# Moving one of four block subtractions from GpSimd to VectorE at the entry of a Strassen-like channel mixer

## The chip, the cores and the metric

The kernel runs on one core of one Trainium2 chip. The time is device microseconds of one execution. Before the change three runs gave 2134.68, 2135.33 and 2136.11 us, a median of 2135.33 us.

## The reference

The kernel computes a two-layer trunk over 1024 positions of width 1024. Layer 0 has a gated spatial mixer, layer 1 has chunked attention, and each layer ends with a gated channel mixer. The output is a final RMSNorm of the residual stream. The change lies in the entry of the channel mixer:

```python
def conv_ffn(h, w_in, conv_w, conv_b, w_down):
    a = h @ w_in
    C = a.shape[-1]
    a = lax.conv_general_dilated(
        a, conv_w[:, None, :].astype(a.dtype), window_strides=(1,),
        padding=[(CONV_WIDTH - 1, 0)], dimension_numbers=('NWC', 'WIO', 'NWC'),
        feature_group_count=C) + conv_b
    up, gate = jnp.split(a, 2, axis=-1)
    return (jax.nn.silu(gate) * up) @ w_down

h = h + conv_ffn(rmsnorm(h, f_norm_g[l]), f_w_in[l], f_conv_w[l], f_conv_b[l], f_w_down[l])
```

Here w_in maps the width of 1024 to 2 x 2816 channels, "up" and "gate".

## The kernel before

**Number format.** Every float32 operand of a matmul is split into a high part (rounded to the TensorE format, cast on ScalarE, L139) and a low part (the rest, a subtraction on VectorE or GpSimd, L140). A product is then three matmuls: high weight by high operand (L375), low weight by high operand (L377), high weight by low operand (L380).

**Seven products for eight.** The channel mixer computes its 2 x 2 block products in the form of Strassen and Winograd. The operand B (the normed residual) has blocks B11, B12, B21, B22: the first digit is the half of the 1024 features, the second the half of the 1024 positions. A block consists of four tiles of 128 features by 512 positions, numbered k = 0 to 3. Three products need sums of blocks: T1 = B12 - B11, T2 = B22 - T1, T3 = B22 - B12 and T4 = B21 - T2. For the weights A, with rows "up" and "gate", the sums S1 to S4 are formed per channel block j on VectorE (L390). One product is one step of twelve matmuls of 128 x 128 by 128 x 512, and seven steps make one channel block j of 128 up and 128 gate channels.

**Which step needs what.** The first channel blocks use plain block products (steps with names such as "A11", "B11"), until the sums of the operand are there. From channel block 2 on the steps are p = 1 to 7, where p = 4 uses T4, p = 5 T1, p = 6 T2 and p = 7 T3. The order is 1, 2, 6, 5, 7, 3 for block 2; then block 3's p = 1; then block 2's p = 4, which is the first step that reads T4; then block 3's 5, 6, 2, 7, 3, and so on. Results gather in PSUM in places called up and gate. Before step p = 4 of a block, ScalarE copies one half of gate to the other (L902) and VectorE adds a saved sum to it (L903); after p = 3 VectorE adds a saved sum to up (L899).

**Behind the products.** A depthwise convolution of width 3 starts on ScalarE (L831) and ends in two operations on VectorE (L833), which read PSUM; ScalarE applies silu (L838) and VectorE multiplies (L839). For each pair of channel blocks GpSimd then forms the four differences T1, T3, T2, T4 of the gated rows (L847), in this order, and SP's queue stores them (L849). The weight loads of later channel blocks (L799) are issued from the same SP queue.

**The entry.** `norm_second` (from L326) norms the second half of the positions, forms T1 and T2 in place of the residual's tiles and splits each operand. Its VectorE work stands in a block whose order is written out by hand: row by row, each row's elementwise work for k followed by the split of k - 1. Function `t2` makes, for each k, T3 (L356) and T2 (L357) on VectorE and T4 (L358) on GpSimd. The splits of T3 and T4 go on a list, `late`, from which the mixer's loop takes two at a time between its steps; the last two, those of T4 for k = 2 and 3, come behind step p = 5 of block 2. Outside the hand-ordered blocks, the order on each engine but TensorE is fixed when the kernel is built, by a planner that works from modelled times. Each engine then runs its instructions in that fixed order.

The two mixers call `norm_second` once each, so L358 runs eight times.

Of the kernel before, what the change touches and what calls it, by code (L numbers as in the profile page):

```python
# [13 lines left out]
ALU = mybir.AluOpType  # L14
# [32 lines left out]
def trunk(ctx: ExitStack, tc: tile.TileContext, x, a_win, a_wv, a_wst, a_bs, a_wout, w_kv, w_q, w_o,  # L47
          f_win, f_wdown, bias, cst, consts, fgain, out):
    nc = tc.nc
    V, S, G = nc.vector, nc.scalar, nc.gpsimd  # L50
# [15 lines left out]
    def put_off(us, fn):  # L66
        pending.append((clock[0] + us, len(pending), fn))
        pending.sort(key=lambda e: e[0])
# [64 lines left out]
    def col(c):  # L133
        return cc[:, c:c + 1]


    def split(hi, lo, src, eng=V):

        behind[S] = S.copy(hi, src)  # L139
        return eng.tensor_tensor(lo, src, f32(hi), op=ALU.subtract)  # L140
# [62 lines left out]
    def spread(r, pool, eng=None):  # L203

        bc = psS("bc")
        if eng is S:
            dg = pool.tile([P, 4, P], F32, tag="f", name="dg")
            for i in range(4):
                S.mul(dg[:, i, :], ident, r[:, i:i + 1])
            nc.tensor.matmul(bc, ones, dg.rearrange("p a b -> p (a b)"), start=True, stop=True)  # L210
            return bc

        rr = pool.tile([P, NB], F32R, tag="st", name="rr")
        split(rr[:, 0:4], rr[:, 4:8], r[:, 0:4])
        for n in range(2):
            dg = pool.tile([P, 4, P], F32R, tag="f", name="dg")
            V.tensor_tensor(dg, ident.unsqueeze(1).broadcast_to([P, 4, P]),
                            f32(rr[:, 4 * n:4 * n + 4]).unsqueeze(2).broadcast_to([P, 4, P]), op=ALU.mult)
            nc.tensor.matmul(bc, ones_r, dg.rearrange("p a b -> p (a b)"), start=n == 0, stop=n == 1)
            tick()  # L220
        return bc
# [20 lines left out]
    def rstd_rows(acc, pool, then, cs=slice(0, H)):  # L242

        pt = psS("pm")
        sums = [acc[0][:, cs], *([acc[1][:, cs]] if len(acc) > 2 and cs.start else []), *acc[2:]]
        n = (cs.stop - cs.start) // P
        for k, a in enumerate(sums):
            for i in range(n):
                nc.tensor.matmul(pt[:, i:i + 1], a[:, i * P:(i + 1) * P], ones[:, 0:1], start=k == i == 0,
                                 stop=k == len(sums) - 1, skip_group_check=True)  # L250
                tick(0)
        then(rstd_of(pt[:, :n], n, pool))
# [73 lines left out]
    def norm_second(h, acc, gain, X, wait=3.6):  # L326

        def scale(r):
            bc = spread(r, npl, S)

            def ys_of(k):
                return [[h[i][:, hs] for hs in halves] for i in (k, k + 4)]

            def part(n, k, new, y, eng=V):
                X[n][k] = b = new()
                split(*b, y, eng)

            def row(work, parts):

                for k, fn in enumerate(work):  # L340
                    fn(k)
                    if k:
                        parts(k - 1)
                parts(len(work) - 1)

            def scaled(k):
                y = h[k][:, halves[1]]
                V.scalar_tensor_tensor(y, y, col(gain + k), bc, op0=ALU.mult, op1=ALU.mult)

            def t1(k):  # L350
                (y11, y12), _ = ys_of(k)
                V.tensor_tensor(y11, y12, y11, op=ALU.subtract)

            def t2(k):
                (y11, y12), (y21, y22) = ys_of(k)
                V.tensor_tensor(y12, y22, y12, op=ALU.subtract)  # L356
                V.tensor_tensor(y22, y22, y11, op=ALU.subtract)  # L357
                G.tensor_tensor(y21, y21, y22, op=ALU.subtract)  # L358

            with tc.manual_schedule(engines={mybir.EngineType.DVE}):  # L360
                row([scaled] * KD, lambda k: part("B22" if k >= 4 else "B12", k % 4, new_y if k >= 4 else new_t,
                                                  h[k][:, halves[1]], G if k % 2 else V))
                row([t1] * 4, lambda k: part("T1", k, new_y, ys_of(k)[0][0]))
                row([t2] * 4, lambda k: part("T2", k, new_t, ys_of(k)[1][1]))
            late.extend(lambda k=k: part("T3", k, new_t, ys_of(k)[0][1]) for k in range(4))
            late.extend(lambda k=k: part("T4", k, new_t, ys_of(k)[1][0]) for k in range(4))
        put_off(wait, lambda: rstd_rows(acc, npl, lambda r: put_off(3.2, lambda: scale(r))))
# [1264 lines left out]
```

## Time and profile before

| what | value |
| --- | --- |
| median of three runs | 2135.33 us |
| span of the profiled execution, first to last instruction | 2131.1 us |
| TensorE busy | 2116.7 us, 99% |
| VectorE busy | 1545.7 us, 73% |
| ScalarE busy | 1065.4 us, 50% |
| GpSimd busy | 752.9 us, 35% |
| mean granted TensorE clock | 0.998 |
| L358 on GpSimd | 8 operations, 27.0 us |

The profile is of one execution. Its engines are PE (TensorE matmuls), PEld (weight loads of TensorE), DVE (VectorE), ACT (ScalarE), POOL (GpSimd) and SP (the queue of transfers). Times in a timeline are microseconds from the start of the span. An entry "[2.72 <-DVE gate L903]" means that the engine stood idle 2.72 us and that VectorE's operation of line 903 ended this. The first channel mixer's entry lies near 300 to 370 us, the second's near 1485 to 1560 us. Spans on GpSimd are rough; they include time in which an operation has started and does not get on.

### The profile page before, as it was taken

To read this page: it belongs to the slowest core of one execution; us is meant where nothing else is said; L and a number is where in the kernel's file an instruction comes from. 1 tells how busy PE (TensorE), PEld (TensorE's weight loads), DVE (VectorE), ACT (ScalarE), POOL (GpSimd) and SP (SyncE) were. 2 spreads that over 40 slices of the span, in tenths; PEclk is the share of its full clock that TensorE was granted. 3 is DMA by queue.
4 is the path that set the end of the run, shared out by engine and by line. 5 is a ranking of instruction groups with operands and counts; after the bars stand their busy time and mean duration, and the time that the engine had idled before them with its cause. 6 is when DMAs were issued, how large, how long until landed. Compare 5 with 4: busy or idle time off the path is not lost.

```text
span 2131.1 us, 28842 instructions
## 1 busy us (share of the span) xinstructions
PE 2116.7 (99%) x9944; PEld 1773.0 (83%) x9944; DVE 1545.7 (73%) x2311; ACT 1065.4 (50%) x1878; POOL 752.9 (35%) x530
## 2 busy tenths in 40 slices
PE   9999999999999999999999999999999999999998
PEld 8888877888888888888888888888888888888887
DVE  4188789888888856675665655665988888885576
ACT  6333555545455544555555555643545544454443
POOL 1075745242333412054545444421322323341020
PEclk9999999999999999999999999999999999999999
DMA  7257722354445976735554555663243545478653
GB/s 253 79 203 256 243 99 99 130 193 138 163 165 194 296 269 215 239 105 139 139 127 129 129 130 133 178 218 114 73 154 134 186 137 175 164 278 300 213 190 126
DMA packets 181450, 367.86 MB, mean 173 GB/s; under 512 B 42908, under 2 KB 43292, under 8 KB 181304
## 3 DMA queue, kind: packets, MB, share of 16 engines
q1 hardware_dynamic: 177128, 358.47, 51.8%
q10 hardware_dynamic: 4176, 7.55, 1.0%
q8 instruction: 78, 1.28, 0.3%
q14 instruction: 68, 0.56, 0.1%
HBM read 233.12 MB, written 103.40 MB: 158 GB/s over the span
## 4 chain that ended last, share of the span: by engine, by line
PE 93%; DVE 4%; POOL 1%; ACT 1%; issue 1%; DMA 0%; DVEq 0%; SPq 0%; POOLq 0%; ACTq 0%
PE up L995 10%; PE gate L995 10%; PE up L375 7%; PE up L377 7%; PE up L380 7%; PE gate L375 5%; PE gate L377 5%; PE gate L380 5%; PE vps L510 4%; PE qkv L184 4%; PE qkv L181 4%; PE qkv L188 4%; PE ups L181 1%; PE po L1290 1%; PE st L1256 1%; PE ups L184 1%
## 5 line engine op out<-in xcount | busy, mean ns | idle before, releaser
L140 DVE TENSOR_TENSOR wlo<-raw,whi 128x512 fp32r<-128x512 f32 (+1 forms) x395 | 343.7, 876 | 179.8 <-ACT whi L139 179.6
L139 ACT CAST whi<-raw 128x512 fp32r<-128x512 f32 (+1 forms) x395 | 245.0, 623 | 282.7 <-PE gate L995 198.5
L375 PE MATMUL up<-yh,whi 128*128 128x512 f32 x688 | 267.8, 389 | 0.0
L377 PE MATMUL up<-yh,wlo 128*128 128x512 f32 x688 | 267.8, 389 | 0.0
L1270 POOL TENSOR_TENSOR pl<-p,ph 128x640 fp32r<-128x640 f32 (+4 forms) x128 | 161.1, 1261 | 180.1 <-ACT ph L1269 134.4
L847 POOL TENSOR_TENSOR h<-a 128x512 f32<-128x512 f32 x44 | 80.6, 1832 | 398.7 <-DVE a L839 387.3
L375 PE MATMUL gate<-th,whi 128*128 128x512 f32 x496 | 193.9, 391 | 2.7 <-DVE gate L903 2.7
L377 PE MATMUL gate<-th,wlo 128*128 128x512 f32 x496 | 193.9, 391 | 0.0
L380 PE MATMUL up<-yl,whi 128*128 128x512 f32 x688 | 184.2, 389 | 0.0
L380 PEld LDWEIGHTS up<-yl,whi 128*128 128x128 f32 x688 | 129.2, 188 | 27.2 <-POOL yl L140 0.5
L375 PEld LDWEIGHTS up<-yh,whi 128*128 128x128 f32 x688 | 129.2, 188 | 27.1 <-ACT gate L886 0.3
L377 PEld LDWEIGHTS up<-yh,wlo 128*128 128x128 f32 x688 | 129.2, 188 | 26.8
L140 DVE TENSOR_TENSOR yl<-raw,yh 128x512 fp32r<-128x512 f32 x172 | 143.1, 834 | 8.4 <-ACT yh L139 8.2
L184 PE MATMUL qkv<-yh,wlo 128*128 128x512 f32 x336 | 134.3, 400 | 0.0
L380 PE MATMUL gate<-tl,whi 128*128 128x512 f32 x496 | 132.7, 389 | 0.0
L181 PE MATMUL qkv<-yh,whi 128*128 128x512 f32 x336 | 132.5, 394 | 0.0
L139 ACT CAST whi<-S 128x512 fp32r<-128x512 f32 x160 | 99.0, 619 | 65.0 <-PE up L380 59.0
L140 DVE TENSOR_TENSOR wlo<-S,whi 128x512 fp32r<-128x512 f32 x160 | 130.2, 814 | 0.0
L995 PE MATMUL up<-yl,whi 128*128 128x512 f32 (+1 forms) x312 | 120.6, 387 | 0.0
L995 PE MATMUL up<-yh,whi 128*128 128x512 f32 (+1 forms) x312 | 120.4, 386 | 0.0
L995 PE MATMUL gate<-yh,wlo 128*128 128x512 f32 (+1 forms) x312 | 120.4, 386 | 0.0
L995 PE MATMUL up<-yh,wlo 128*128 128x512 f32 (+1 forms) x312 | 120.3, 386 | 0.0
(306 smaller groups left out, 5274.6 us busy)
## 6 DMA issues: line engine op xcount, KB each, us to landing
raw<-in_f_win SPq DMA_DIRECT2D x88, 512.0 KB
gT<-h SPq DMA_DIRECT2D x88, 256.0 KB
h<-in_f_wdown SPq DMA_DIRECT2D x44, 512.0 KB
dS<-h SPq DMA_DIRECT2D x88, 256.0 KB
raw<-dS SPq DMA_DIRECT2D x40, 512.0 KB
raw<-gT SPq DMA_DIRECT2D x40, 512.0 KB
gB<-a SPq DMA_DIRECT2D x66, 256.0 KB
raw<-in_f_wdown SPq DMA_DIRECT2D x30, 512.0 KB
```

Of the source, the lines that this page charges most:

```text
L139: behind[S] = S.copy(hi, src)
L140: return eng.tensor_tensor(lo, src, f32(hi), op=ALU.subtract)
L181: nc.tensor.matmul(ps, wh[:, k, :], xs[k][0], start=k == 0, stop=False)
L184: nc.tensor.matmul(ps, wl[:, k, :], xs[k][0], start=False, stop=False)
L188: nc.tensor.matmul(ps, wh[:, k, :], xs[k][1], start=False, stop=k == last)
L375: nc.tensor.matmul(ps, wh[:, k, :], xs[k][0], start=first and k == 0, stop=False, skip_group_check=True)
L377: nc.tensor.matmul(ps, wl[:, k, :], xs[k][0], start=False, stop=False, skip_group_check=True)
L380: nc.tensor.matmul(ps, wh[:, k, :], xs[k][1], start=False, stop=k == 3, skip_group_check=True)
L510: nc.tensor.matmul(ps, a, b, start=k == i == 0, stop=k == KD - 1 and i == 2)
L847: G.tensor_tensor(B[n], x, B.get(y) if isinstance(y, str) else y, op=ALU.subtract)
L995: nc.tensor.matmul(ps[:, cs], w[:, ms], x[:, cs], start=q == i == 0 and p in (1, 6, 5, 4), stop=q == NP - 1 and i == 2, skip_group_check=True)
L1270: marks[2] = G.tensor_tensor(pl[:, :n], pf[:, :n], f32(ph[:, :n]), op=ALU.subtract)
```

## The change

T4 of the last tile, k = 3, is subtracted on VectorE. Those of k = 0, 1 and 2 stay on GpSimd. Since `t2` is called inside the hand-ordered block, the new VectorE operation stands directly behind T2's of k = 3 (L357) and ahead of the splits of T2 for k = 2 and k = 3. Nothing else is edited.

```diff
                 V.tensor_tensor(y12, y22, y12, op=ALU.subtract)
                 V.tensor_tensor(y22, y22, y11, op=ALU.subtract)
-                G.tensor_tensor(y21, y21, y22, op=ALU.subtract)
+                (V if k == 3 else G).tensor_tensor(y21, y21, y22, op=ALU.subtract)
```

## Prediction, made before the changed kernel was run

> **What bounds the kernel now.** I read the page's busy shares first, then the waits of TensorE (PE) over the whole run (engine, line, what it waited for; total, times, longest).
>
> ```profile
> span 2131.1 us, 28842 instructions
> PE 2116.7 (99%) x9944; PEld 1773.0 (83%) x9944; DVE 1545.7 (73%) x2311; ACT 1065.4 (50%) x1878; POOL 752.9 (35%) x530
> ...
> PE gate L375 <- DVE gate L903: 2.7, 1, 2.7
> PE gate L249 <- DVE acc L238: 1.0, 1, 1.0
> ```
>
> TensorE is busy nearly all the time, so a change can only win what TensorE waits, plus what its clock loses over a wait. One wait stands out, and it is in the stage that this change edits: it lies in the first channel mixer, before VectorE's L903. The chain of waits around it (start, length, what) leads back to the changed line, L358:
>
> ```profile
> 342.76 8.32 POOL h L358
> ...
> 355.25 0.62 PE gate L375
> ```
>
> The timeline of each engine (start, length, engine, line, operation; in brackets the idle time before it and who ended it) gives the way from the one to the other.
>
> ```profile
> 333.37 5.76 POOL L358 TENSOR_TENSOR h<-h,h 128x512 f32<-128x512 f32 x1 [1.39 <-DVE h L357]
> 342.71 8.36 POOL L358 TENSOR_TENSOR h<-h,h 128x512 f32<-128x512 f32 x1
> ...
> 345.15 0.62 ACT L139 CAST th<-h 128x512 fp32r<-128x512 f32 x1
> 351.10 0.62 ACT L139 CAST th<-h 128x512 fp32r<-128x512 f32 x1 [5.33 <-POOL h L358]
> 352.15 0.58 ACT L902 COPY gate<-gate 128x512 f32<-128x512 f32 x1
> ...
> 349.24 0.69 DVE L390 TENSOR_TENSOR S<-raw,S 128x512 f32<-128x512 f32 x1
> 351.75 1.14 DVE L140 TENSOR_TENSOR tl<-h,th 128x512 fp32r<-128x512 f32 x1 [1.83 <-ACT th L139]
> 352.82 1.77 DVE L140 TENSOR_TENSOR wlo<-raw,whi 128x512 fp32r<-128x512 f32 x1
> 354.51 0.69 DVE L903 TENSOR_TENSOR gate<-gate,h 128x512 f32<-128x512 f32 x1
> 355.11 1.18 DVE L140 TENSOR_TENSOR wlo<-S,whi 128x512 fp32r<-128x512 f32 x1
> 356.21 0.69 DVE L899 TENSOR_TENSOR up<-up,h 128x512 f32<-128x512 f32 x1
> ```
>
> The subtraction of k = 3, the one that moves, sits 8.36 us on GpSimd (POOL). ScalarE stands 5.33 us in front of the cast of its result, and behind that cast in ScalarE's queue stand a weight cast and L902, the turn of the gate's sums. VectorE stands 1.83 us, then does the low part, a weight's low part and L903, and only then may TensorE take the product of T4. TensorE's own rows, and windows with its busy time, granted clock, DMA share and GB/s in the last columns:
>
> ```profile
> 349.65 0.39 PE L375 MATMUL up<-yh,whi 128*128 128x512 f32 x1
> 355.25 0.62 PE L375 MATMUL gate<-th,whi 128*128 128x512 f32 x1 [2.72 <-DVE gate L903]
> 359.69 0.40 PE L375 MATMUL up<-yh,whi 128*128 128x512 f32 x1
> 367.86 0.39 PE L375 MATMUL gate<-th,whi 128*128 128x512 f32 x1
> ...
> 293.00:296.40 3.40, 2.58 (x15) 2.32 (x16) 2.00 (x4) 0.36 (x2) 1.02 (x1) 1.00 0.12 25
> 355.25:359.00 3.75, 3.75 (x10) 2.93 (x10) 2.93 (x5) 1.20 (x1) 0.48 (x1) 0.54 0.81 247
> ```
>
> From 359.69 to 367.86 lie three products, 2.72 us each. The product of T4 should therefore start at 349.65 + 2.72 = 352.37 and the next at 355.09. It starts at 355.25 and the next at 359.69. **The stall costs 359.69 - 355.09 = 4.60 us**: 2.88 us of waiting and 1.72 us because the product behind it runs at a granted clock of 0.54. The wait of 1.0 us at L249 cost no clock: its window shows 1.00.
>
> **Why GpSimd takes 8.36 us.** The same kind of operation, beside other work of VectorE:
>
> ```profile
> L358 POOL TENSOR_TENSOR h<-h,h x8: 1633/2277/8361, 325.0 to 1522.5; 128x512 f32<-128x512 f32 x8
> ...
> 340.00:350.00 10.00, 10.00 (x46) 8.26 (x45) 9.93 (x15) 5.16 (x10) 10.00 (x2) 1.00 0.12 45
> ...
> 336.09 0.69 DVE L357 TENSOR_TENSOR h<-h,h 128x512 f32<-128x512 f32 x1
> 337.89 1.28 DVE L833 SCALAR_TENSOR_TENSOR a<-gate,cc,a 128x1023 f32<-128x1023 f32 x1
> 340.29 1.29 DVE L140 TENSOR_TENSOR tl<-h,th 128x512 fp32r<-128x512 f32 x2
> 347.50 1.22 DVE L839 TENSOR_TENSOR a<-a 128x1024 f32<-128x1024 f32 x1
> ...
> 351.04 1.31 POOL L847 TENSOR_TENSOR h<-a 128x512 f32<-128x512 f32 x1
> 352.31 3.42 POOL L847 TENSOR_TENSOR h<-a,h 128x512 f32<-128x512 f32 x2
> ```
>
> VectorE is busy 9.93 of 10 us there. The subtraction of k = 2 (333.37) ends at 339.13, together with L833 (337.89 to 339.17), whose source lies in PSUM; the one of k = 3 ends 1.1 us after VectorE fell idle at 349.93. So GpSimd gets through while VectorE does not read two SBUF operands, and needs 1.1 to 1.2 us of such time. The reverse shows too: the weight's low part at 352.82 takes 1.77 us in place of 0.69 while L847 runs.
>
> **The change, part by part.** *Removed*: GpSimd's operation of k = 3, twice in the run (once per mixer). No DMA hangs on it. ScalarE's cast at 351.10 can then follow the one at 345.15, at 345.7, and L902 waits only for TensorE's product of T3, which ends two products ahead of the natural start of T4's: 352.37 - 2 x 2.72 = 346.93.
>
> *Added*: one subtraction on VectorE behind L357 of k = 3. The same kind, L357, takes 0.69 us and the next instruction follows 0.60 later; I take 0.60. VectorE's stream from there to 349.93 has no gap, so everything behind it moves by 0.60. Two things feel it.
>
> First, the low part of T2's k = 3 (first of the two at 340.29) ends at 341.58 in place of 340.98. TensorE wants it for the last of these four matmuls, at 340.56 + 3 x 0.23 = 341.25:
>
> ```profile
> 340.56 1.08 PE L380 MATMUL gate<-tl,whi 128*128 128x512 f32 x4
> ```
>
> With 0.04 us from a VectorE end to a matmul (355.20 to 355.25) that is a **new wait of 0.37 us**; the bounds are 0 (the stream recovers) and 0.60 (no slack at all). It is too short for the clock, by the 1.0 us row.
>
> Second, L903. VectorE reaches 349.84 (349.24 + 0.60), does the sum S, the low part of T4's k = 3, a weight's low part, and starts L903 at 349.84 + 3 x 0.60 = 351.64, ending 352.33. TensorE, 0.37 later than its rhythm, wants it at 352.74: no wait, with 0.4 us to spare. The bounds are a wait of 0 and of 0.8 (two more instructions of 0.60 in front).
>
> *What is late next*: GpSimd's three differences of L847 (T3, T2, T4 of the gated rows) now meet the full VectorE. T3 needs L839, which ends at 349.3. It comes through during L903 (source in PSUM), 351.7 to 352.8, T2 during L899, which follows L903 by one weight's low part (the rows at 355.11 and 356.21), about 353.4 to 354.5, T4 when VectorE next runs dry, by 356.9. SP's queue issues T3's store and, behind it, a weight load:
>
> ```profile
> 352.37 0.32 SPq L849 DMA_DIRECT2D gT<-h  x1
> 354.61 0.33 SPq L799 DMA_DIRECT2D raw<-in_f_win  x1
> ...
> 358.90 0.69 DVE L390 TENSOR_TENSOR S<-raw 128x512 f32<-128x512 f32 x1 [0.82 <-DMA raw<-in_f_win]
> 363.69 0.68 DVE L140 TENSOR_TENSOR wlo<-S,whi 128x512 fp32r<-128x512 f32 x1
> ```
>
> The load is issued at about 353.2, 1.4 earlier, and S starts at 357.5; the weight at 363.69 follows 4.79 later and ends at 363.0. TensorE wants it at 367.86 - 4.23 + 0.23 = 363.9. It holds, with 0.9 us; bounds 0 and 0.5 of wait.
>
> *The second mixer* has the operation too:
>
> ```profile
> 1522.47 2.28 POOL L358 TENSOR_TENSOR h<-h,h 128x512 f32<-128x512 f32 x1 [1.32 <-DVE h L357]
> ...
> 1523.65 2.18 DVE L839 TENSOR_TENSOR a<-a 128x1024 f32<-128x1024 f32 x1
> 1540.63 0.69 DVE L903 TENSOR_TENSOR gate<-gate,h 128x512 f32<-128x512 f32 x1
> ...
> 1542.31 0.39 PE L375 MATMUL gate<-th,whi 128*128 128x512 f32 x1
> ```
>
> There TensorE never waits: L903 ends at 1541.32, 0.99 us ahead of need. VectorE gains 0.96 (L839 takes 2.18 beside GpSimd, 1.22 alone) and pays 0.60. Its cover is those 0.99 us, so the term is 0, with bounds 0 and 0.6.
>
> **Sum**: -4.60 + 0.37 = **-4.23 us**. The span goes from 2131.1 to 2126.9. The runs' median lies 4.2 above the span, and I carry that over: 2135.33 - 4.23 = 2131.1. A change of 0.2% (4.27 us) is about what a measurement of this kernel can tell from none, and the forecast lies on that line.
>
> **Rivals.**
>
> *The clock did not drop in the timed runs.* The 1.72 us come from one execution. Only one wait in the middle of the run lost clock, so how often a gap of 2.88 us does so isn't shown; the runs' spread of 1.4 us has about this size. Then the gain is 2.88 - 0.37 = 2.5: 2132.8. The Trainium skill, "TensorE: Matmul & The Clock Gate", section "What's actually happening", gives a free-running window of about 3.4 us and half rate after an idle one; by it a gap of 2.88 us would drop the clock only in some positions, which speaks for this rival, while the row here shows that it did drop.
>
> *GpSimd takes the port in between.* If T3, ready at 349.3, gets in at the next instruction boundary and T2 behind it, each holds VectorE for 1.14 us (1.77 - 0.69 shows 1.08). L903 ends at 354.6 in place of 352.33, TensorE waits 1.9: 2133.0, or 2134.7 with a clock loss. For it: the stretched rows at 351.75 and 352.82. Against: the whole 7.2 us up to 349.93, in which GpSimd waited at every boundary. The Trainium skill, "SBUF — State Buffer", section "Who interferes with whom", has whoever issues first hold the pair for a whole instruction; it names no right of VectorE to keep it over a run of instructions, as the trace shows.
>
> *The stall moves ten us on.* If T3 gets nothing during L903 and L899, it waits until VectorE runs dry at about 354.7 and ends at 355.9; the load behind it in SP's queue is issued at 356.0 and lands at 360.2, the weight is ready at 365.6 in place of 363.0, and TensorE waits 365.6 - 363.9 = 1.7: 2132.8. Against: L903 reads PSUM as L833 does.
>
> *Slower.* The order outside the hand-ordered blocks is laid by a planner from modelled times, and the edit changes these. If it puts L903 behind the two weights' low parts that now follow it, GpSimd's three differences hold VectorE there: 351.64 + 2 x 0.60 + 3 x 1.14 = 356.3, against 354.51 now, 1.8 us worse than before; in the second mixer, laid by the same planner, 4.6 - 0.99 = 3.6 us of new wait and 1.7 of clock. Together 7.1: 2142.4. It decides from the point where L903 of the first mixer starts after 354.51. For it: VectorE has no slack here. Against: L903 hangs on an event of TensorE that is not moved.
>
> *It does nothing.* If another wait stands right behind the one removed (L902 or the load of a weight), the time stays within 1 us of 2135.3. Against: no row shows one.
>
> **How the numbers follow.** Forecast 0.55, clock 0.12, port 0.09, moved stall 0.08, nothing 0.06, slower 0.10. The forecast's own gain, from its bounds, is 3.2 to 4.8. The line of 4.27 us lies inside it: 0.40 of its 0.55 I put beyond it, since the new wait of 0.37 has a bound at 0 and VectorE's other terms err to both sides. So faster 0.40, slower 0.10, and within 0.2% the remaining 0.15 of the forecast and the four cases of less gain, 0.50. The range of 8 in 10 leaves out the slower case and a little of the last one, and reaches 1.1 us below the forecast for the bounds and the runs' spread: 2130.0 to 2135.4.
>
> **What would show it.** Right: no operation of L358 on GpSimd from 340 on; ScalarE's casts of T4 without the 5.33 us; L903 of the first mixer ending near 352.3; no TensorE wait over 1 us there and a granted clock of 1.00 through 350 to 360; a wait of some 0.4 us at L380 near 341. Wrong: L903 after 353, a TensorE wait near 364, L847 starting long before L903 and VectorE rows of 1.7 us around it, or a wait in the second mixer near 1542.

## The result, and the profile after

The changed kernel takes **2131.62 us**, the median of 11 runs (2130.22 to 2133.61). Eleven runs of the kernel before, taken with them, have a median of 2135.33 us. The ratio is 0.9979, with a 95% interval of 0.9971 to 0.9988, which is 2.6 to 6.2 us less. The two medians differ by 3.71 us. The forecast was 2131.1, the range 2130.0 to 2135.4.

The page's first lines, and the waits of TensorE over the whole run after the change (engine, line, what it waited for; total, times, longest):

```profile
span 2129.5 us, 28843 instructions
PE 2116.1 (99%) x9944; PEld 1771.8 (83%) x9944; DVE 1546.9 (73%) x2313; ACT 1066.3 (50%) x1878; POOL 744.6 (35%) x528
...
PE gate L249 <- DVE acc L238: 1.0, 1, 1.0
...
PE up L375 <- ACT gate L886: 0.6, 1, 0.6
...
PE gate L380 <- DVE tl L140: 0.2, 1, 0.2
```

The wait of 2.7 us before L903 is gone. One at L380 is new, and it is the only one left between 320 and 420 us. The rest of the difference lies outside the changed stage; the largest new row there, 0.6 us at L886, is taken up below.

To measure the stage itself, take the first matmul of block 2's p = 1 (330.58 before) and the first of block 3's p = 5 (359.69 before). Between them lie nine products, and 9 x 2.72 = 24.48 us is their length without a wait. TensorE's timeline, first before, then after the change (start, length, engine, line, operation; in brackets the idle time ahead of it and what ended it):

```profile
330.58 0.39 PE L375 MATMUL up<-yh,whi 128*128 128x512 f32 x1
```

```profile
331.71 0.39 PE L375 MATMUL up<-yh,whi 128*128 128x512 f32 x1
...
342.78 0.50 PE L380 MATMUL gate<-tl,whi 128*128 128x512 f32 x1 [0.25 <-DVE tl L140]
...
354.02 0.39 PE L375 MATMUL gate<-th,whi 128*128 128x512 f32 x1
...
356.74 0.39 PE L375 MATMUL up<-yh,whi 128*128 128x512 f32 x1
```

The stage took 359.69 - 330.58 = 29.11 us before and takes 356.74 - 331.71 = 25.03 us after, **4.08 us less**. What is left above 24.48 is 0.55 us, nearly all of it at L380. (The stage starts 1.13 us later in this execution; a second execution of the kernel before starts it at 333.06, later still, so the start differs from execution to execution. Places in the stage are compared from its start.)

VectorE's, ScalarE's, GpSimd's and SP's timelines around the place where the stall was:

```profile
349.26 1.21 DVE L839 TENSOR_TENSOR a<-a 128x1024 f32<-128x1024 f32 x1
350.40 0.67 DVE L390 TENSOR_TENSOR S<-raw,S 128x512 f32<-128x512 f32 x1
351.00 1.28 DVE L140 TENSOR_TENSOR tl<-h,th 128x512 fp32r<-128x512 f32 x2
352.20 0.67 DVE L140 TENSOR_TENSOR wlo<-raw,whi 128x512 fp32r<-128x512 f32 x1
352.80 0.68 DVE L903 TENSOR_TENSOR gate<-gate,h 128x512 f32<-128x512 f32 x1
353.40 1.19 DVE L140 TENSOR_TENSOR wlo<-S,whi 128x512 fp32r<-128x512 f32 x1
354.52 0.68 DVE L899 TENSOR_TENSOR up<-up,h 128x512 f32<-128x512 f32 x1
355.12 1.19 DVE L140 TENSOR_TENSOR wlo<-S,whi 128x512 fp32r<-128x512 f32 x1
356.24 1.79 DVE L140 TENSOR_TENSOR wlo<-raw,whi 128x512 fp32r<-128x512 f32 x1
358.58 0.69 DVE L390 TENSOR_TENSOR S<-raw 128x512 f32<-128x512 f32 x1 [0.55 <-DMA raw<-in_f_win]
...
347.25 1.15 ACT L139 CAST th<-h 128x512 fp32r<-128x512 f32 x2
...
348.81 0.59 ACT L902 COPY gate<-gate 128x512 f32<-128x512 f32 x1
...
350.61 3.44 POOL L847 TENSOR_TENSOR h<-a 128x512 f32<-128x512 f32 x1 [4.90 <-DVE a L839]
354.01 3.47 POOL L847 TENSOR_TENSOR h<-a,h 128x512 f32<-128x512 f32 x2
...
354.08 0.32 SPq L849 DMA_DIRECT2D gT<-h  x1
354.49 0.38 SPq L799 DMA_DIRECT2D raw<-in_f_win  x1
```

ScalarE's two casts of T4 stand together at 347.25 with no idle time, and L902 comes at 348.81 in place of 352.15. VectorE runs on without a gap. L903 ends at 353.48, 0.54 us ahead of the product at 354.02. GpSimd's L847 stands from 350.61 and gets on only with L903; the stretched rows of VectorE (1.19, 1.19, 1.79) all lie behind L903. The window from 351.00 to 354.50, in which the stall would have come, has TensorE busy 3.50 of 3.50 us at a granted clock of 1.00.

**Where the rest is.** The stage wins 4.08 us, but the spans of the two profiled executions differ by 1.6 only. Outside the stage, waits of half a microsecond come and go. The largest such step after the change, on TensorE:

```profile
1753.25 0.50 PE L375 MATMUL up<-yh,whi 128*128 128x512 f32 x1 [0.56 <-ACT gate L886]
```

VectorE had waited 3.65 us for a weight's transfer just ahead of it. This lies nearly 200 us behind the second mixer's entry. The second executions below speak against the edit as its cause: the kernel before has a wait of 0.42 us at this row's place in its second one (1758.74), and the changed kernel has none in its second. Outside the stage (span less stage) the two executions of the kernel before take 2102.0 and 2106.2 us, the two of the changed kernel 2104.5 and 2104.8. So two spans can't judge a change of 4 us. One small cost is the edit's: the stretch of the second mixer from block 2's p = 1 to the T4 product's low parts behind it. Its first matmul starts at 1490.63 before and 1488.09 after, the last row of low parts at 1563.18 before and 1560.82 after. That is 72.55 us before and 72.73 after, 0.18 longer, with no wait on any matmul's row.

### The profile page after: what moved, and what is told of

It is laid out like the page before. It is cut to its first block, busy times and chain, and to the rows that moved or that the text cites. A ratio compares the mean times of both kernels' runs of the same rounds, so it can differ in the third digit from the quotient of the medians.

```text
span 2129.5 us, 28843 instructions
## 1 busy us (share of the span) xinstructions
PE 2116.1 (99%) x9944; PEld 1771.8 (83%) x9944; DVE 1546.9 (73%) x2313; ACT 1066.3 (50%) x1878; POOL 744.6 (35%) x528
## 4 chain that ended last, share of the span: by engine, by line
PE 93%; DVE 4%; ACT 1%; issue 1%; DMA 0%; POOL 0%; SPq 0%; DVEq 0%; POOLq 0%; ACTq 0%
PE up L995 10%; PE gate L995 10%; PE up L375 7%; PE up L377 7%; PE up L380 7%; PE gate L375 5%; PE gate L380 5%; PE gate L377 5%; PE vps L510 4%; PE qkv L184 4%; PE qkv L181 4%; PE qkv L188 4%; PE ups L181 1%; PE po L1290 1%; PE st L1256 1%; PE po L1288 1%
## 5 line engine op out<-in xcount | busy, mean ns | idle before, releaser
L847 POOL TENSOR_TENSOR h<-a 128x512 f32<-128x512 f32 x44 | 82.0, 1864 | 403.3 <-DVE a L839 390.7
L380 PE MATMUL up<-yl,whi 128*128 128x512 f32 x688 | 184.2, 389 | 0.0
L380 PEld LDWEIGHTS up<-yl,whi 128*128 128x128 f32 x688 | 129.1, 188 | 27.3 <-POOL yl L140 0.5
L380 PE MATMUL gate<-tl,whi 128*128 128x512 f32 x496 | 132.8, 389 | 0.2 <-DVE tl L140 0.2
```

Of the source, the lines that this page charges most:

```text
L380: nc.tensor.matmul(ps, wh[:, k, :], xs[k][1], start=False, stop=k == 3, skip_group_check=True)
L847: G.tensor_tensor(B[n], x, B.get(y) if isinstance(y, str) else y, op=ALU.subtract)
```

## The experiments

Each comparison below is with runs of the kernel before on the same chip. "Stage" is the length defined above: 29.11 us before, 25.03 after. "Second stretch" is that of the second mixer: 72.55 and 72.73.

**One mixer at a time.** L358 runs in both mixers; these two kernels make the edit in one of them only.

```diff
-                (V if k == 3 else G).tensor_tensor(y21, y21, y22, op=ALU.subtract)
+                (V if k == 3 and gain == C_FG else G).tensor_tensor(y21, y21, y22, op=ALU.subtract)
```

> T4 of k = 3 goes to VectorE in the first mixer only. If the gain comes from the stall before L903 in the first mixer (my theory), the whole gain is here: 3.7 to 4.1 us below the kernel before, a wait of about 0.4 us at L380 near 342 us, no wait before L903. If the changed order in the second mixer brings part of it (rival), the gain is smaller by over 1 us.

```diff
-                (V if k == 3 else G).tensor_tensor(y21, y21, y22, op=ALU.subtract)
+                (V if k == 3 and gain != C_FG else G).tensor_tensor(y21, y21, y22, op=ALU.subtract)
```

> T4 of k = 3 goes to VectorE in the second mixer only; the first mixer is as before. My theory: no gain, within 0.7 us of the kernel before, and the stall of 2.7 us with its half-rate clock is still there in the first mixer. Rival (the second mixer shares in the gain, or pays part of it back): 1 us or more to either side, with a TensorE wait that appears or disappears after 1490 us.

The first mixer alone: 2131.07 us against 2135.78, ratio 0.9977 [0.9968, 0.9986]; stage 25.03, second stretch 72.56. The second alone: 2135.58 against 2135.78, ratio 0.9995 [0.9986, 1.0004]; stage 29.12, second stretch 72.72, and TensorE waits 2.7 us for L903 as of old.

The whole gain is in the first mixer. The second mixer's half of the edit is worth nothing; the traces show it 0.16 to 0.20 us slower in all three executions that have it, and the times can't tell that from zero.

**Is it the engine or the order?** The theory says that GpSimd's last T4 was not slow in itself, but held off by VectorE for as long as no instruction let it through. Then GpSimd can keep the operation if it only comes ahead of L847's T1, so that it meets L833, which reads PSUM. Every other engine's order is that of before.

```diff
-                G.tensor_tensor(y21, y21, y22, op=ALU.subtract)
+                behind["t4"] = G.tensor_tensor(y21, y21, y22, op=ALU.subtract)
...
-                G.tensor_tensor(B[n], x, B.get(y) if isinstance(y, str) else y, op=ALU.subtract)
+                with tc.issue_after(behind["t4"].ins) if j == 1 and n == "T1" else ExitStack(): G.tensor_tensor(B[n], ...)
```

> All four T4 stay on GpSimd. Only two GpSimd instructions change places: T4 of k = 3 in front of T1 of the gated rows (L847). Every other engine keeps its order. Port theory: T4 then starts at about 339.1 and ends with the convolution step of VectorE at 342.7, ScalarE's wait of 5.3 us is gone and so is the stall of 4.6 us; T1 is held off in its place until L903, SP's store of T1 delays the weight load behind it, and TensorE waits 0.8 us (0 to 1.5) one weight later, near 363: a gain of 3.8 us (3.1 to 4.6). Rival (the gain needs VectorE's new order, or the operation itself is slow on GpSimd): the stall stays, a gain under 1 us.

2133.14 us against 2135.78, ratio 0.9985 [0.9976, 0.9995]. TensorE's, GpSimd's and VectorE's rows:

```profile
332.49 0.39 PE L375 MATMUL up<-yh,whi 128*128 128x512 f32 x1
...
356.99 0.39 PE L375 MATMUL up<-yh,whi 128*128 128x512 f32 x1
...
366.10 0.50 PE L377 MATMUL gate<-th,wlo 128*128 128x512 f32 x1 [0.56 <-DVE wlo L140]
...
368.77 0.39 PE L375 MATMUL up<-yh,whi 128*128 128x512 f32 x1
...
335.33 9.36 POOL L358 TENSOR_TENSOR h<-h,h 128x512 f32<-128x512 f32 x2 [1.38 <-DVE h L357]
344.66 9.60 POOL L847 TENSOR_TENSOR h<-a 128x512 f32<-128x512 f32 x1
...
343.46 1.27 DVE L833 SCALAR_TENSOR_TENSOR a<-gate,cc,a 128x1022 f32<-128x1022 f32 x1
```

The stage is 356.99 - 332.49 = 24.50 us: the stall is gone without moving anything to VectorE. T4 of k = 3 ends at 344.69, with L833 (343.46 to 344.73), and now T1 of L847, the same kind of operation, is held for 9.60 us in its place. Nothing on TensorE waits for T1, but SP's queue does: the weight load behind T1's store comes late, and the product with the wait at 366.10 takes 3.62 us (365.15 to 368.77) in place of 2.72, 0.90 more, about as expected. Another 0.96 us at 396.75 was not expected; the second execution of the changed kernel loses 0.50 at the same matmul, so its cause stays open. The stage wins 29.11 - 24.50 = 4.61, and 2.75 is left of that, as the medians say (2.64); the gain expected was 3.1 to 4.6. The cause of the stall is settled all the same: the held operation, not GpSimd's own work, and it matters only which operation is the one that is held.

**Behind the splits.** The forecast's new wait at L380 comes from the low part of T2 that the added subtraction pushes back. Here the subtraction stands behind T2's splits and ahead of T4's.

```diff
-                (V if k == 3 else G).tensor_tensor(y21, y21, y22, op=ALU.subtract)
+                k < 3 and G.tensor_tensor(y21, y21, y22, op=ALU.subtract)
...
-                row([t2] * 4, lambda k: part("T2", k, new_t, ys_of(k)[1][1]))
+                row([t2] * 4, lambda k: part("T2", k, new_t, ys_of(k)[1][1])); V.tensor_tensor(ys_of(3)[1][0], *ys_of(3)[1], op=ALU.subtract)
```

> T4 of k = 3 on VectorE as in the changed kernel, but behind the low part of T2's k = 3 in place of ahead of it. If the 0.4 us wait at L380 is the price of the 0.6 us put in front of that low part, the wait is gone and the gain is 4.6 us, 0.4 to 0.5 more than the changed kernel's, L903 still in time. If the wait has another cause, it stays at 0.4 us.

2130.92 us against 2135.78, ratio 0.9974 [0.9964, 0.9984]. TensorE and VectorE:

```profile
332.90 0.39 PE L375 MATMUL up<-yh,whi 128*128 128x512 f32 x1
342.88 1.08 PE L380 MATMUL gate<-tl,whi 128*128 128x512 f32 x4
...
357.61 0.39 PE L375 MATMUL up<-yh,whi 128*128 128x512 f32 x1
...
342.66 0.68 DVE L140 TENSOR_TENSOR tl<-h,th 128x512 fp32r<-128x512 f32 x1
343.27 0.68 DVE L364 TENSOR_TENSOR h<-h,h 128x512 f32<-128x512 f32 x1
```

The four matmuls of L380 run without a gap, and the stage is 24.71 us, 0.32 less than in the changed kernel, where 0.4 to 0.5 was expected; the second stretch is 72.54. What is left above 24.48 lies at the product of T4: L903 ends at 354.70, and the product starts at 354.76, 0.1 late. So VectorE's spare time ahead of L903 is used up. The two stretches together are 0.5 us shorter than in the changed kernel. That is below what the times can tell; the kernel is clearly faster than the kernel before.

**More blocks.** If VectorE's stream has room, more of T4 could move: k = 2 and 3, or all four.

```diff
-                (V if k == 3 else G).tensor_tensor(y21, y21, y22, op=ALU.subtract)
+                (V if k >= 2 else G).tensor_tensor(y21, y21, y22, op=ALU.subtract)
```

> T4 of k = 2 and k = 3 on VectorE, both ahead of the low part of T2's k = 3. Theory: two times 0.60 us in front of that low part, a wait of 0.9 to 1.0 us at L380 near 342 in place of 0.37, no stall before L903: 3.5 us faster than the kernel before, 0.6 slower than the changed one. Rival (GpSimd relieved further is a gain in itself): faster than the changed kernel.

2133.53 us against 2136.70, ratio 0.9988 [0.9978, 0.9997]. TensorE's waits from 320 to 420, VectorE's and GpSimd's rows, and a window with its granted clock (0.62) ahead of the last two columns:

```profile
PE gate L380 <- DVE tl L140: 1.9, 2, 1.2
...
336.74 1.80 DVE L140 TENSOR_TENSOR tl<-h,th 128x512 fp32r<-128x512 f32 x1
...
336.37 1.63 POOL L847 TENSOR_TENSOR h<-a 128x512 f32<-128x512 f32 x1 [3.87 <-DVE a L839]
...
344.60:348.30 3.70, 3.69 (x10) 2.88 (x11) 3.70 (x6) 3.10 (x5) 0.00 (x0) 0.62 0.03 7
```

The waits at L380 are 1.9 us, about twice what I had expected. GpSimd, relieved of k = 2, is free when L839 ends, gets the port, and stretches a low part from 0.68 to 1.80. In this execution one of the waits also cost a piece of half clock, and the stage is 29.09, no shorter than before. The median is 3.2 us lower all the same, near the 3.5 that was expected, but this trace doesn't show where: the profiled execution took 2133.06 us because it was quick outside the stage (2102.0 us, like the first one of the kernel before). If both kernels spend alike outside, most timed runs had a shorter stage than this one; how often the clock drops there isn't shown. The agreement with the 3.5 is of the number, not of the mechanism.

```diff
-                (V if k == 3 else G).tensor_tensor(y21, y21, y22, op=ALU.subtract)
+                V.tensor_tensor(y21, y21, y22, op=ALU.subtract)
```

> All four T4 on VectorE. Theory: four times 0.60 us in front of the low part, 2.4 - 0.23 = a wait of about 2.2 us at or before L380 near 342, with a half-rate clock behind it if the gap is seen: 0.7 to 2.4 us faster than the kernel before. Rival (the port relieved for good): as fast as the changed kernel or faster.

2139.77 us against 2136.70, ratio 1.0013 [1.0004, 1.0023]: 3.1 us **slower** where 0.7 to 2.4 faster was expected, a miss. TensorE's waits from 320 to 420, and a window:

```profile
PE gate L380 <- DVE tl L140: 2.2, 2, 1.7
PE gate L375 <- ACT th L139: 2.0, 1, 2.0
...
350.00:354.00 4.00, 4.00 (x10) 3.10 (x10) 4.00 (x7) 2.14 (x4) 1.23 (x1) 0.50 0.13 47
```

Three waits for T2's parts, 4.2 us together, come in place of the one at L903, the clock is halved for 6.83 us from 347.26 on, and the stage is 32.09. The second mixer waits 1.3 us at L380 as well. I had counted 0.60 us for each further operation. But the last T2 (L357 of k = 3) comes 4.80 us later in the stage than in the kernel before (343.67 - 333.36 against 336.09 - 330.58), and three further operations are only 1.8 of these. The rest is other VectorE work that now stands ahead of it, in an order that the planner chose. VectorE runs without a gap here, so the stage can take little more than one operation of 0.60 us.

**A gap in the port.** The sharpest test of the port: leave T4 on GpSimd, and put one more VectorE operation that reads PSUM into VectorE's stream while T4 is held. It should let T4 through there.

```diff
-            late.extend(lambda k=k: part("T4", k, new_t, ys_of(k)[1][0]) for k in range(4))
+            late.extend(lambda k=k: (part("T4", k, new_t, ys_of(k)[1][0]), k == 0 and gain == C_FG and V.tensor_tensor(psum["gate"][1][:, 0:H], psum["gate"][1][:, 0:H], ys_of(0)[1][0], op=ALU.add)) for k in range(4))
```

> All four T4 stay on GpSimd and GpSimd's order stays. VectorE gets one more instruction in the first mixer, of no use: like L903 it reads one operand from PSUM and one from SBUF, on a PSUM place that is overwritten before it is read again, behind the low part of T4's k = 0. Port theory: GpSimd's T4 of k = 3, held off since 342.7, gets through beside it, ends at about 347.5 in place of 351.0, VectorE pays 0.60 for the instruction and up to 0.55 for the one behind it, L903 ends at 352.9 against a need at 352.4: a wait of about 0.5 us in place of 2.9, and 4.0 us faster than the kernel before, by work added. Rival (GpSimd is slow for another reason): T4 still ends at 351 or later, L903 is no earlier, and the kernel is 0 to 0.6 us slower.

2137.37 us against 2135.74, ratio 1.0008 [0.9999, 1.0016]. GpSimd, VectorE (L366 is the added operation), ScalarE, TensorE, and the window behind the wait:

```profile
345.44 4.81 POOL L358 TENSOR_TENSOR h<-h,h 128x512 f32<-128x512 f32 x1
352.68 1.63 POOL L847 TENSOR_TENSOR h<-a 128x512 f32<-128x512 f32 x1 [2.43 <-DVE a L839]
...
349.02 0.69 DVE L366 TENSOR_TENSOR gate<-gate,h 128x512 f32<-128x512 f32 x1
349.62 1.18 DVE L140 TENSOR_TENSOR tl<-h,th 128x512 fp32r<-128x512 f32 x1
...
353.07 1.80 DVE L390 TENSOR_TENSOR S<-raw,S 128x512 f32<-128x512 f32 x1
354.79 1.77 DVE L140 TENSOR_TENSOR tl<-h,th 128x512 fp32r<-128x512 f32 x1
356.48 1.75 DVE L140 TENSOR_TENSOR wlo<-raw,whi 128x512 fp32r<-128x512 f32 x1
358.15 0.69 DVE L903 TENSOR_TENSOR gate<-gate,h 128x512 f32<-128x512 f32 x1
...
350.28 0.62 ACT L139 CAST th<-h 128x512 fp32r<-128x512 f32 x1 [1.78 <-POOL h L358]
...
358.89 0.80 PE L375 MATMUL gate<-th,whi 128*128 128x512 f32 x1 [3.64 <-DVE gate L903]
...
358.89:362.50 3.61, 3.61 (x10) 2.90 (x11) 2.33 (x4) 1.21 (x1) 0.00 (x0) 0.60 0.76 226
```

The first half is as expected. T4 comes through beside L366, in 4.81 us in place of 8.36, the row behind L366 is stretched to 1.18, and ScalarE waits 1.78 in place of 5.33. The second half is not (4.0 us faster was expected, and the interval includes no change at all): T3, T2 and T4 of L847 then get the port one after the other between VectorE's instructions, each of the three rows ahead of L903 takes 1.75 to 1.80 us, and TensorE waits 3.64 for L903. That is the rival "GpSimd takes the port in between" of the prediction, real in this kernel though not in the changed one.

**Second executions**, to see what repeats: the kernel before, the gap, and the changed kernel.

> The kernel before, unchanged, for a second trace. If the half-rate clock follows from the 2.9 us gap every time, the stall costs 4.6 us again with one half-rate stretch. If it depends on where the gap falls, it costs between 2.9 and 4.6 us. Steps of up to 0.7 us elsewhere against the first trace are differences from execution to execution, and show what of the small steps between the traces of before and after is not due to the change.

> The kernel of e8 once more, for a second trace. In e8 GpSimd's three differences (L847) got the port between VectorE's instructions from 353 on and stretched three of them by 1.1 us each; in the changed kernel they waited for L903. If this belongs to the order of the instructions, the same three rows are 1.75 us or longer again and TensorE waits 3.4 to 3.8 us before L903; if it is chance in the arbitration, other rows are stretched, or none, and the wait is 0.3 to 2.5 us.

> The changed kernel once more, for a second trace. If the order decides who gets the port, VectorE's rows between the second L839 and L903 of the first mixer last 0.67 us each again, and the wait at L380 near 342 is 0.25 us of record (0.47 us of delay), with no wait before L903. If it is chance, L903 can be late by 1.1 us or a multiple, and the changed kernel has executions with a stall.

The kernel before: 2137.46 us, stage 29.15, second stretch 72.56, a wait of 2.8 us at L903 with a granted clock of 0.54 behind it. It also has waits elsewhere that its first profile lacks (0.31 us near 219, 0.79 near 1567, 0.42 near 1759). The wait of 1.0 us at L249, which cost no clock in the first profile, does here. Its window:

```profile
296.00:299.80 3.80, 3.80 (x11) 2.97 (x10) 0.28 (x2) 1.89 (x5) 1.02 (x1) 0.55 0.47 138
```

The gap again: 2134.52 us, with the same three stretched rows (1.79, 1.78, 1.75) and the same wait of 3.64. Both executions of this order agree, and so do all three of the changed kernel's order in the first mixer, so it is the order of the instructions that decides who gets the port here, and hardly chance. The clock did **not** drop this time, and the stage is 28.46 in place of 29.78. TensorE's row and the window behind it:

```profile
357.58 0.50 PE L375 MATMUL gate<-th,whi 128*128 128x512 f32 x1 [3.64 <-DVE gate L903]
...
357.58:361.00 3.42, 3.42 (x15) 2.84 (x16) 2.34 (x4) 1.51 (x2) 0.00 (x0) 1.00 0.79 241
```

The changed kernel: 2131.90 us, stage 25.03, second stretch 72.75, the wait of 0.2 at L380, no stretched row ahead of L903. It repeats to 0.02 us.

## Why the prediction was right, point by point

**The stall and its cause: right.** It was put at 4.60 us. The stage was 29.11 - 24.48 = 4.63 us over its length without a wait, and all of this but the new wait at L380 is gone. The cause, GpSimd's operation held off by VectorE's stream, is shown by two experiments that leave the operation on GpSimd: earlier in GpSimd's order it is not held past L833, and with a PSUM-reading operation put beside it, it comes through there. The chain from it through ScalarE's cast and L902 to L903 holds as well: in the gap kernel, ScalarE's wait shrank with it (5.33 to 1.78).

**The new wait at L380: right in kind, sized too small.** Forecast 0.37 us, bounds 0 and 0.60. The three matmuls ahead of it start at 341.69 and follow each other at 0.23, so the last was due at 341.69 + 3 x 0.23 = 342.38; it starts at 342.78, 0.40 late. But the next matmul then follows 0.34 later (343.12) in place of 0.23: TensorE takes another 0.11 to get going again, which the forecast left out. Together some 0.5 us.

**"Too short for the clock, by the 1.0 us row": the number held, the reason didn't.** The clock stayed at 1.00 behind this wait. But the 1.0 us row at L249 is no proof: the same wait halved the clock in 4 of the 12 profiled executions. I read a rule from one execution; what decides is worked out in the last section.

**L903 in time: right.** Forecast: its end 21.75 us from the stage's start (352.33 - 330.58), no wait. Measured: 353.48 - 331.71 = 21.77, with 0.54 to spare.

**What is late next: right.** T3 of L847 came with L903, T2 with L899. T4 came 0.5 us earlier than "when VectorE runs dry", stretching the low part at 356.24 to 1.79. The load was to be issued 22.6 us from the stage's start and S to start at 26.9; measured 22.8 and 26.9. The weight behind it caused no wait.

**The second mixer: 0 forecast, 0.18 measured**, inside its bounds of 0 and 0.6. No matmul's row shows a wait; two products take 2.77 and 2.85 us in place of 2.72. Why isn't settled. L839 takes 1.23 us, as forecast, but VectorE now waits 0.66 us ahead of it for ScalarE's silu (L838), a wait that the forecast left out. L903 ends 0.80 us ahead of need (1539.03 for 1539.83) in place of 0.99, and still causes no wait.

**The sum.** -4.60 + 0.37 = -4.23 forecast; in the traces -4.08 in the stage and +0.18 in the second mixer, -3.90; the medians differ by 3.71, the ratio says 4.5 with an interval of 2.6 to 6.2.

**Span and median.** The prediction carried over that the median lay 4.2 us above the profiled span. In every later run, of any of these kernels, the execution's own time is 1.8 to 2.6 us above its span, 2.1 in the middle. So the other 2.1 of the 4.2 meant that the profiled execution of before was itself a quick one, at about 2133.2. The predicted span of 2126.9 was therefore too low (2129.5), while the predicted median came out right because the shift was applied to the median.

**The rivals.** *The clock did not drop in the timed runs*: three profiled executions with a gap of 2.7 to 2.9 us all dropped, so 2.9 us alone isn't what was won; but a 3.64 us gap did and did not, so the 1.72 us are a likelihood, not a constant. By the limit worked out in the last section, 2.08 of the 2.88 us would have to lie in one piece of 3.41 us. If every position is equally likely, that is so about six times in ten (an estimate), so the rival was likelier than its 0.12. *GpSimd takes the port in between*: not here, but in the gap kernel. *The stall moves on*: not here; in the kernel with GpSimd's order changed it does, at 0.90 us. *Slower by the planner*: it did lay VectorE's instructions otherwise ahead of L903 (four low parts stand together at 342.05, and the last two of T4 at 351.00), but L903 kept its place. *Nothing*: the experiment with the first mixer alone rules it out.

**Open.** T3 of L847 starts 0.14 us behind L839's end in both kernels, yet in the changed kernel it loses every boundary up to L903, and in the gap kernel it wins the second. The orders of VectorE behind L839 are S, low, low, weight, L903 in the one and low, S, low, weight, L903 in the other. In the kernel with two blocks moved, T1 wins the first boundary behind its start too. Why the order decides was not settled.

## What to carry to other kernels

When an operation on GpSimd takes several times its usual length, ask first what VectorE was doing beside it: reordering GpSimd's own queue, so that the operation meets a VectorE instruction that reads PSUM, removed the same stall as moving the work did. Moving one operation of 0.60 us onto an engine that runs without a gap pays if it ends a wait of several us, and the next three of the same kind made the kernel slower: count the slack of what stands behind the new place, operation by operation. Put the moved operation behind what is needed first, and judge the edit by the length of its own stage, since half-microsecond waits elsewhere hid more than 2 us of 4 in the span.

## What the runs showed of the hardware that was not expected

**The clock.** In the middle of a run, a halved stretch lasted 3.41 us wherever it came, or twice that (6.83, in the kernel with four blocks moved). Whether a gap brings one is not set by its length alone: 2.7 to 2.9 us dropped 3 of 3 times, 3.64 us 1 of 2, and the wait of 1.0 us 4 of 12. The clock records of the twelve traces, read together, show what does. Counted from the clock's first rise, 3.9 to 10.2 us into the span, every drop starts at a whole multiple of 3.413 us. So the run is cut into pieces of this length, and they fall on the program differently in each execution. Count 0.227 us of work from the start of a matmul of 512 columns (the distance of two of them), and less for fewer columns in proportion. Then work fills 4% to 38.8% of the ten pieces just ahead of a drop, and 39.0% or more of each of some 7400 other pieces at full clock (the ends of a run aside: in a first piece, 29% brought no drop). The 3.64 us gap dropped the clock when 3.13 us of it lay in one piece, and not when 1.92 and 1.72 lay in two. Behind the wait of 1.0 us stand eight matmuls of one column (L249, 0.9 us); the clock dropped in just the four executions in which the wait and these matmuls lay in one piece. The limit was found in these traces and has been tried on no others.

The Trainium skill, "TensorE: Matmul & The Clock Gate", section "What's actually happening", has a free-running window of 3413 ns, and the traces agree with that length; its condition of a whole idle window they don't bear out, since 1.0 us of waiting was enough four times. Nor can a gap of 2.88 us fill a window of that length, so the prediction's "only in some positions" doesn't follow from that condition; it follows from the pieces above. Halved stretches, which cost 1.6 us behind L249 and 1.7 behind L903, probably make much of the spread of the runs. Of 65 runs of the kernel before, the 19 with a mean granted clock of 0.997 or less average 2136.8 us, the 37 at 0.998 2136.0, the 9 at 0.999 2135.2; that shows the link, not the share.

**The port.** VectorE's back-to-back instructions with two SBUF operands kept GpSimd waiting over many instruction boundaries: 8.36 us for the held T4, 9.60 for the held T1 in the kernel with the other order, against 1.63 for an operation that got in. The held operations got in where VectorE stood idle or read PSUM. That is not the whole rule: in the gap kernel and in the one with two blocks moved, an operation that started right behind L839 got in between two instructions that read SBUF alone. Once in, GpSimd took every second turn in the gap kernel: each of its three operations held VectorE's next one for 1.1 us (1.80, 1.77, 1.75 in place of 0.68).
